# Weight halves written by two DMAs in layer A and in the second block

## The chip, the cores and the metric

The kernel runs on one core of a Trainium2 chip. The metric is the device time of one execution in microseconds (us); of a kernel that was run several times the median counts.

The engines and the letters of the profile: PE is TensorE (matrix products; PEld is its loading of stationary operands), DVE is VectorE, ACT is ScalarE, POOL is GpSimd, SP is SyncE, which here only issues DMAs. A DMA that an engine issues stands in that engine's queue and moves data by itself; SP's DMAs go through queue q1 (hardware_dynamic on the page), GpSimd's through q0 (software_dynamic).

## The reference, cut to what matters

One sequence of S = 512 tokens of width D = 1024, float32 throughout, goes through three blocks:

```
def first_block(x, ...):                       # DEPTH = 2
    for i in range(2):
        mix = dsa_mixer(h, ...) if i == 0 else gla_mixer(h, ...)       # layer A, layer B
        h = layer_norm(DN_ALPHA * h + mix, ...)
        h = layer_norm(DN_ALPHA * h + square(relu(h @ w_up)) @ w_down, ...)   # MLP0, MLP1

def dsa_mixer(x, ...):                         # layer A
    proj = x @ w_in                            # 1024 x 2120: q, k, v, iq, ik, iw
    ... rotate q, k, iq, ik; score = sum_h iw * relu(iq . ik); keep the 128 best keys of each query
    p = softmax(q . k over the kept keys);  o = p @ v
    return o @ w_o                             # 1024 x 1024

def second_block(x, c, ...):
    h = modulate(rms_norm(x), ...)
    proj = h @ w_in                            # 1024 x 2832: q, k, v, mLSTM q and k, v, o, gates
    y_attn = axial attention(q, k, v);  y_mem = bidirectional mLSTM(...)
    x = x + g1 * (concatenate([y_attn, y_mem]) @ w_out)                # 1024 x 1024
    x = x + g2 * ((silu(h @ w_gate) * (h @ w_up)) @ w_down)            # the FFN
    return rms_norm(x)
```

`dsa_mixer`'s two matrices and `second_block`'s `w_in` and `w_out` are the ones that the change touches.

## The kernel before, in words

TensorE's fast path takes a rounded float32 (F32R). To keep float32 precision each operand `x` of a projection is held as two rounded parts, `hi = round(x)` and `lo = x - hi`, and a projection is three products: `hi*hi + hi*lo + lo*hi`. The activations' parts are `xT_hi` and `xT_lo` (line names), the weights' parts `wh` and `wl`.

A weight load takes a tile of 128 partitions x 2048 columns (1 MB; some are smaller) in three steps. SP issues a DMA of the raw float32 weights into a buffer of tag "raw" (name `wr`; L129 in `wcols`, L104 in `wraw`, which `wheads` uses for `w_o` and `w_out`). Then `wsplit` (L107) works in two pieces: ScalarE copies the raw weights to F32R (`wh`, L88), VectorE subtracts (`wl = wr - wh`, L85). The tags raw, wh and wl have two buffers each. As soon as a load's split has read its raw buffer, the next load but one can be fetched into it: raw weights lie ready some time before the split can run, and the split waits for a free pair `wh`, `wl`, that is until PE has made the last product with the pair's load before.

The program runs layer A (`layer_a`, L457), MLP0, layer B (`gla`, `gate_out`), MLP1, the second block (`second`, L1005) and its `ffn`. In layer A the projections are run as steps (`proj_steps`, L146): tokens in 4 tiles of 128, two at a time, and the 1024 rows of the weights in 2 loads of 512 rows; iq's columns first (its first load comes with x through `load_x`), then k with ik and iw (328 columns, "k chunk" below), V (256), Q0 and Q1 (512 each), interleaved with index scores, the selection and attention; at the end `w_o` in 4 loads. The second block does likewise: VM (mLSTM's v), AQ, KV (272 columns), C (four loads of 256 columns, all 1024 rows), OG, then `w_out` in 4 loads.

The order of the instructions on each engine is fixed before the run by a scheduler, from priorities and from when it reckons that operands are there. What stands under `net.urgent()` (loads and splits) gets priority over everything else, in program order among itself. An engine then works its list strictly in order: what stands behind an instruction that waits, waits too. That holds for the DMA issues of SP and of GpSimd as well.

Of the kernel before, what the change touches and what calls it, by code (L numbers as in the profile page):

```python
# [10 lines left out]
F32 = mybir.dt.float32  # L11
F32R = mybir.dt.float32r
I32 = mybir.dt.int32
AF = mybir.ActivationFunctionType
ALU = mybir.AluOpType
# [11 lines left out]
P = 128  # L27
# [10 lines left out]
class Net:  # L38
    def __init__(self, ctx, tc, ins, out):
        self.tc, self.nc, self.ins, self.out = tc, tc.nc, ins, out  # L40
        nc = self.nc
        self.cp = ctx.enter_context(tc.tile_pool(name="cp", bufs=1))
        self.wp = ctx.enter_context(tc.tile_pool(name="wp", bufs=2))
        self.sp = ctx.enter_context(tc.tile_pool(name="sp", bufs=4))
        self.pp = ctx.enter_context(tc.tile_pool(name="pp", bufs=2, space=PSUM))
        self.new_xt()
        self.xh = self.cp.tile([P, KB, S], F32R, name="xT_hi")
        self.xl = self.cp.tile([P, KB, S], F32R, name="xT_lo")
        self.ident = self.cp.tile([P, P], F32, name="ident")
        make_identity(nc, self.ident)  # L50
        self.identr = self.cp.tile([P, P], F32R, name="identr")
        nc.vector.tensor_copy(self.identr, self.ident)
        self.epst = {}
        self.nurgent = 0

    def new_xt(self):
        self.xt = self.cp.tile([P, NT, D], F32, tag="xt", name="x_tok")
# [37 lines left out]
        return self.pp.tile([P, 512], dt, tag=tag, bufs={"a": 3, "t": 2, "s": 2, "o": 1}[tag], name="ps_" + tag)  # L95


    def wraw(self, srcs, kb, n, name="w"):

        with self.urgent():  # L100
            raw = self.wp.tile([P, 2048], F32, tag="raw", name=name + "r")[:, : kb * n]
            rv = raw.rearrange("p (k n) -> p k n", k=kb)
            for psl, ap in srcs:
                self.nc.sync.dma_start(rv[psl], ap)  # L104
        return raw, rv
# [15 lines left out]
    def wcols(self, w, r0, kb, cols):  # L121

        n = sum(m for _, m in cols)
        with self.urgent():
            raw = self.wp.tile([P, 2048], F32, tag="raw", name="wr")[:, : kb * n]
            rv = raw.rearrange("p (k n) -> p k n", k=kb)
            o = 0
            for c0, m in cols:
                self.nc.sync.dma_start(rv[:, :, o : o + m], w[r0 : r0 + kb * P, c0 : c0 + m].rearrange("(k p) n -> p k n", p=P))  # L129
                o += m  # L130
        return self.wsplit(raw, kb, n)

    def wchunk4(self, w, r0, c0):
        return self.wchunk(w, r0, 4, c0, 512)

    def wheads(self, w, r0, c0):

        raw, _ = self.wraw([(slice(64 * b, 64 * b + 64), w[r0 + b * 256 : r0 + b * 256 + 256, c0 : c0 + 512]
                             .rearrange("(r d) n -> d r n", d=64)) for b in range(2)], 4, 512)
        return self.wsplit(raw, 4, 512)  # L140

    def proj_tok(self, *args, **kw):
        for _ in self.proj_steps(*args, **kw):
# [312 lines left out]

def layer_a(net, first):  # L457
    nc, tc, I = net.nc, net.tc, net.ins
    w_in, w_o = I["a_w_in"][0], I["a_w_o"][0]
    xk = net.xk()  # L460
    with tc.tile_pool(name="da", bufs=1) as da:
# [6 lines left out]
        v = da.tile([P, NT, 4, 64], F32, name="v")  # L468
# [175 lines left out]
def mlp(net, i, extra, mod=None):  # L644

    nc, tc, I = net.nc, net.tc, net.ins
    w_up, w_dn = I["mlp_w_up"][i], I["mlp_w_down"][i]
    with tc.tile_pool(name="ml", bufs=1) as mp:
        st = mp.tile([P, NT, 2, 6], F32, name="st")
        hid, rows = [], []  # L650
        NG = 8

        def hidden():
            hid.append([mp.tile([P, 2, S], F32R, tag=x, name=x, bufs=3) for x in ("hh", "hl")])
            return hid[-1]

        def ev_up(j, ps):
            hh, hl = hidden() if j % 2 == 0 else hid[-1]
            r = mp.tile([P, S], F32, tag="eo", name="relu", bufs=2)
            nc.scalar.activation(r, ps, AF.Relu)  # L660
            nc.scalar.activation(r, r, AF.Square)
            net.split(hh[:, j % 2, :], hl[:, j % 2, :], r)

        def up(c):
            e = net.proj_seven(mp, w_up, c * 256, xs, AF.Relu)
            hh, hl = hidden()
            for v, sc in ((e[:, 1], 1.0), (e[:, 2:4], -1.0)):
                nc.scalar.activation(v, v, AF.Relu, scale=sc)
            nc.scalar.activation(e, e, AF.Square)
            v = e.rearrange("p (f t) n -> p f (t n)", f=2)  # L670
            net.split(hh, hl, v)

        def ev_dn(c, n, t, ps):
            sl = slice(n * 512, (n + 1) * 512)
            x = net.xt[:, t, sl]
            if c == 0:
                nc.vector.scalar_tensor_tensor(x, x, ALPHA, ps, op0=ALU.mult, op1=ALU.add)
            else:
                nc.vector.tensor_tensor(x, x, ps, op=ALU.add)
            if c == 2 * NG - 2:  # L680
                net.ln_stats(net.xt[:, t, :], st[:, t], n)
                if n == 1:
                    net.ln_tile(net.xt[:, t, :], st[:, t], t, rows[0][:, 0], rows[0][:, 1], mod is None)
                    if mod is not None:
                        rms_mod(net, mp, t, rows[0][:, 2], rows[0][:, 3], hm=rows[1][:, t], jtag="eo")

        net.proj_pairs([(w_up, 2 * i * P, lambda b, ps, i=i: ev_up(2 * i + b, ps)) for i in range(2)])
        xs = net.x_sums(mp)
        net.proj_feat(w_up, 512, 2, ev_up)
        for g in range(1, NG):  # L690
            if g > 1:
                up(2 * g)
            for n in range(2):
                down_half(net, w_dn, 2 * g - 2, 2 * g, n, hid, ev_dn)
            up(2 * g + 1)
            if g in (1, 3, 5):
                extra[g // 2](mp)
        rows += [mp.tile([P, NT, D], F32, tag=tag, name="rows_" + tag) for tag in ("th", "tl")]
        for n, r in enumerate([I["ln_mlp_g"][i], I["ln_mlp_b"][i]] + [net.mod[m] for m in mod or ()]):
            net.bcast_row(rows[0][:, n], r)  # L700
        down_last(net, mp, w_dn, 2 * NG - 2, hid, ev_dn)
# [3 lines left out]
def layer_b(net):  # L705
# [14 lines left out]
def gla(net, y, ssq):  # L720
# [284 lines left out]
def second(net):  # L1005
# [2 lines left out]
    w_in, w_out = I["w_in_2"][0], I["w_out_2"][0]  # L1008
    H = 4
    xk = net.xk()  # L1010
    with tc.tile_pool(name="sm", bufs=1) as sm:
        qk = sm.tile([P, 8, S], F32, name="mqk")
        v1 = sm.tile([P, NT, H, P + 2], F32, name="mv")
# [6 lines left out]
        with tc.tile_pool(name="sa", bufs=1) as sa:  # L1020
# [3 lines left out]
            v = sa.tile([P, NT, 2, 64], F32, name="av")  # L1024
# [498 lines left out]
```

## Time and profile before

| | us |
|---|---|
| median of 3 runs | 1858.94 (1856.1 to 1861.33) |
| the profiled execution | 1859.66 |
| its span in the profile | 1857.9 |
| PE busy | 1815.5 (98%) |
| DVE busy | 1440.5 (78%) |
| ACT busy | 912.3 (49%) |
| POOL busy | 19.0 (1%) |

The span runs from the first to the last instruction of the execution; 1.8 us of the execution lie around it. Layer A takes the span's first 245 us or so, MLP0 begins at 251, the second block's mixing runs from about 1190 to 1497. In the rows below, an instruction's row gives its start, its duration, engine, line, operation, `output<-inputs`, shape, type, and `xN` where N like ones follow each other directly; `[0.59 <-ACT hst L88]` is idle time ahead of it and what ended that. Windows give the busy time of each engine in a stretch with the number of instructions, then PE's granted clock as a share of full speed, the DMA engines' busy share and GB/s.

### The profile page before, as it was taken

The page shows a single profiled execution, that of the slowest core. Times are in us where ns is not written, and L with a number is a line of the kernel's source. Part 1 is how long each engine was busy: PE and PEld are TensorE (multiplying, and loading weights), DVE is VectorE, ACT ScalarE, POOL GpSimd, SP SyncE. Part 2 cuts the span into 40 slices and gives each one's busy share as a digit, 9 for nine tenths or more (in the row PEclk, how much of TensorE's full clock was granted, in tenths as well). Part 3 has the DMA queues.
Part 4 walks back from the last instruction along what each step waited for, and adds up shares of the span by engine and source line. Part 5 has one row for each costly group of instructions (what it writes and reads, how often), then busy time and mean ns, then how long its engine had stood idle before and what let it go on. Part 6 is the DMA issues. An engine that isn't in the chain of part 4 may idle for free.

```text
span 1857.9 us, 26802 instructions
## 1 busy us (share of the span) xinstructions
PE 1815.5 (98%) x10564; PEld 1532.8 (83%) x10564; DVE 1440.5 (78%) x2467; ACT 912.3 (49%) x1600; POOL 19.0 (1%) x46
## 2 busy tenths in 40 slices
PE   8999999999999999999999999999999899999997
PEld 7865698988888888889888888777566689999996
DVE  5998589878678587468988777877876787788877
ACT  5568644444443544334544444445677445344334
POOL 0010000000000100000000000000000000000000
PEclk9999999999999999999999999999999999999999
DMA  4231244634324222126454323422112122333232
GB/s 143 91 68 52 67 139 158 207 117 148 103 91 134 61 69 69 68 91 188 140 180 140 113 92 111 139 73 81 46 41 69 45 91 68 114 114 114 79 104 91
DMA packets 127161, 190.80 MB, mean 103 GB/s; under 512 B 9279, under 2 KB 77835, under 8 KB 127036
## 3 DMA queue, kind: packets, MB, share of 16 engines
q1 hardware_dynamic: 126996, 189.03, 32.0%
q8 instruction: 83, 1.36, 0.3%
q14 instruction: 42, 0.34, 0.1%
q0 software_dynamic: 32, 0.07, 0.0%
q10 hardware_dynamic: 8, 0.00, 0.0%
HBM read 186.96 MB, written 2.12 MB: 102 GB/s over the span
## 4 chain that ended last, share of the span: by engine, by line
PE 92%; DVE 5%; ACT 2%; issue 0%; DMA 0%; POOL 0%; SPq 0%; DVEq 0%; ACTq 0%; POOLq 0%
PE ps_a L77 51%; PE ps_s L77 15%; PE ps_t L77 11%; PE ps_o L77 7%; PE ps_t L443 1%; PE ps_t L302 1%; PE ps_s L806 1%; PE ps_a L1275 1%; DVE wl L85 1%; PE ps_t L405 1%; PE ps_s L1241 1%; ACT prob L434 0%; PE ps_s L843 0%; PE ps_o L858 0%; ACT wh L88 0%
## 5 line engine op out<-in xcount | busy, mean ns | idle before, releaser
L88 ACT ACTIVATE wh<-wr 128x1024 fp32r<-128x1024 f32 (+2 forms) x284 | 258.6, 958 | 239.3 <-PE ps_t L77 113.3
L85 DVE TENSOR_TENSOR wl<-wr,wh 128x1024 fp32r<-128x1024 f32 (+2 forms) x284 | 304.1, 1104 | 84.6 <-ACT wh L88 55.1
L77 PE MATMUL ps_a<-wh,xT_hi 128*128 128x512 f32 (+3 forms) x536 | 205.3, 387 | 3.6 <-ACT xT_hi L88 2.2
L77 PE MATMUL ps_a<-wh,xT_lo 128*128 128x512 f32 (+3 forms) x536 | 204.3, 385 | 0.6 <-DVE xT_lo L85 0.6
L88 ACT ACTIVATE wsh<-wr 128x1024 fp32r<-128x1024 f32 x94 | 97.5, 1059 | 184.3 <-DVE wr L254 155.5
L77 PE MATMUL ps_a<-xT_hi,wh 128*128 128x256 f32 (+1 forms) x528 | 163.4, 321 | 0.9 <-DVE gtok L1097 0.5
L77 PE MATMUL ps_a<-xT_lo,wh 128*128 128x256 f32 (+1 forms) x528 | 162.7, 319 | 0.0
L77 PE MATMUL ps_a<-xT_hi,wl 128*128 128x256 f32 (+1 forms) x528 | 147.0, 319 | 0.0
L77 PE MATMUL ps_a<-wl,xT_hi 128*128 128x512 f32 (+3 forms) x536 | 143.6, 381 | 0.0
L77 PE MATMUL ps_s<-wh,hh 128*128 128x512 f32 x344 | 136.6, 397 | 0.1
L77 PE MATMUL ps_s<-wh,hl 128*128 128x512 f32 x344 | 136.7, 397 | 0.0
L77 PE MATMUL ps_a<-tl,wsh 128*128 128x256 f32 x528 | 132.1, 283 | 0.0
L77 PE MATMUL ps_a<-th,wsh 128*128 128x256 f32 x528 | 132.1, 282 | 0.0
L77 PEld LDWEIGHTS ps_a<-wh,xT_hi 128*128 128x128 f32 x536 | 101.5, 189 | 25.0 <-issue 4.5
L85 DVE TENSOR_TENSOR wsl<-wr,wsh 128x1024 fp32r<-128x1024 f32 x94 | 113.0, 1221 | 10.7 <-ACT wsh L88 10.7
L77 PEld LDWEIGHTS ps_a<-wh,xT_lo 128*128 128x128 f32 x536 | 101.5, 189 | 19.8 <-DVE xT_lo L85 1.4
L77 PE MATMUL ps_t<-wh,hl 128*128 128x512 f32 x296 | 117.4, 397 | 0.0
L77 PE MATMUL ps_t<-wh,hh 128*128 128x512 f32 x296 | 117.4, 396 | 0.0
L77 PEld LDWEIGHTS ps_a<-wl,xT_hi 128*128 128x128 f32 x536 | 95.6, 188 | 19.3 <-issue 1.6
L77 PEld LDWEIGHTS ps_a<-xT_hi,wh 128*128 128x128 f32 x528 | 100.1, 190 | 9.3 <-issue 0.8
L77 PEld LDWEIGHTS ps_a<-xT_lo,wh 128*128 128x128 f32 x528 | 100.0, 189 | 7.8 <-issue 0.8
L77 PEld LDWEIGHTS ps_a<-tl,wsh 128*128 128x128 f32 x528 | 100.3, 190 | 0.0
(437 smaller groups left out, 4122.3 us busy)
## 6 DMA issues: line engine op xcount, KB each, us to landing
wr<-in_mlp_w_up_dram SPq DMA_DIRECT2D x32, 1024.0 KB
wr<-in_mlp_w_down_dram SPq DMA_DIRECT2D x32, 1024.0 KB
mod_raw<-in_w_ada_dram SPq DMA_DIRECT2D x48, 512.0 KB
wr<-in_b_w_in_dram SPq DMA_DIRECT2D x12, 1024.0 KB
wr<-in_w_gate_dram SPq DMA_DIRECT2D x11, 1024.0 KB
wr<-in_w_up_dram SPq DMA_DIRECT2D x11, 1024.0 KB
wr<-in_w_in_dram SPq DMA_DIRECT2D x10, 1024.0 KB
wr<-in_w_down_dram SPq DMA_DIRECT2D x10, 1024.0 KB
```

What stands on the lines that cost most here:

```text
L77: self.nc.tensor.matmul(ps, lt, rt, start=first, stop=last)
L85: (eng or self.nc.vector).tensor_tensor(out, x, hi.bitcast(F32), op=ALU.subtract)
L88: self.nc.scalar.activation(out, x, AF.Copy)
L302: self.nc.tensor.transpose(ps[:, j * P : (j + 1) * P], src[:, j * P : (j + 1) * P], self.ident)
L405: nc.tensor.transpose(ps[:, j * P : (j + 1) * P], st[:, j0 + j, :], net.identr)
L443: nc.tensor.transpose(pst[:, kb * P : (kb + 1) * P], pr[:, kb * P : (kb + 1) * P], net.ident)
L806: nc.tensor.matmul(ps[:, c * 64 : c * 64 + 64], x[:, c * C : (c + 1) * C], xv[:, c * m : (c + 1) * m, 1, :], start=True, stop=True)
L1241: nc.tensor.matmul(ps, qk[:, 4 + h, a * P : (a + 1) * P], qk[:, h, :], start=True, stop=True)
L1275: nc.tensor.matmul(o, ws[a][:, b * P : (b + 1) * P], v1[:, a, h, 0:129], start=n == 0, stop=n == len(as_) - 1)
```

## The change

`wcols` and `wheads` now hand their sources to a new function `wload`. Where `net.adding` is false it does what was done before. Where it is true, GpSimd issues a DMA that reads the float32 weights from DRAM and writes them as F32R to `wh` (L113); ScalarE writes `-wh` to `wl` in one instruction (L114); GpSimd issues a second DMA that reads the same weights from DRAM again and adds them to `wl` (L116). SP and VectorE have no part. Two of three such loads take their pair from the tags wh and wl; each third takes both from the tag raw, which such loads no longer need for raw weights: three pairs in turn.

```diff
+    def wload(self, srcs, kb, n):
+        v = lambda x: x.rearrange("p (k n) -> p k n", k=kb)
+        with self.urgent():
+            if not self.adding:
+                raw = self.wp.tile([P, 2048], F32, tag="raw", name="wr")[:, : kb * n]
+                for psl, cs, ap in srcs:
+                    self.nc.sync.dma_start(v(raw)[psl, :, cs], ap)
+                return self.wsplit(raw, kb, n)
+
+            self.nadd += 1
+            wh, wl = (self.wp.tile([P, 2048], F32R, tag="raw" if self.nadd % 3 == 0 else x, name=x)[:, : kb * n] for x in ("wh", "wl"))
+            for psl, cs, ap in srcs:
+                self.nc.gpsimd.dma_start(v(wh)[psl, :, cs], ap)
+            self.nc.scalar.activation(wl, wh.bitcast(F32), AF.Copy, scale=-1.0)
+            for psl, cs, ap in srcs:
+                self.nc.gpsimd.dma_start(v(wl)[psl, :, cs], ap, accum_op=ALU.add)
+        return v(wh), v(wl)
...
     def wcols(self, w, r0, kb, cols):
-        with self.urgent():
-            raw = self.wp.tile([P, 2048], F32, tag="raw", name="wr")[:, : kb * n]
...
-                self.nc.sync.dma_start(rv[:, :, o : o + m], w[r0 : r0 + kb * P, c0 : c0 + m].rearrange("(k p) n -> p k n", p=P))
-        return self.wsplit(raw, kb, n)
+            srcs.append((slice(None), slice(o, o + m), w[r0 : r0 + kb * P, c0 : c0 + m].rearrange("(k p) n -> p k n", p=P)))
+        return self.wload(srcs, kb, n)
...
     def wheads(self, w, r0, c0):
-        raw, _ = self.wraw(...)
-        return self.wsplit(raw, 4, 512)
+        return self.wload(...)
...
 def layer_a(net, first):
+    net.adding = True
...
 def mlp(net, i, extra, mod=None):
+    net.adding = False
...
 def second(net):
+    net.adding = True
...
 def ffn(net):
+        net.adding = False
```

`mlp` sets the flag to false ahead of layer B and nothing sets it to true there, so layer B's loads are as before. Changed are 29 loads: 13 of layer A (all but the first of iq) and 16 of the second block. VectorE's list goes from 2421 to 2363 instructions, ScalarE's from 1467 to 1438, SP's from 317 to 278, GpSimd's from 51 to 129; loads with two sources (k, KV, `w_o`, `w_out`) need two DMAs for each half.

The order on SP, from its first DMAs to MLP0's first loads (`wr_243` is iq's second load, `wr_369` and `wr_404` the k chunks; `wr_2901` and `wr_2911` MLP0's first two); before:

```order
L1423 DMA x_tok_67<-in_x_dram 128x512 x6
L129 DMA wr_243<-in_a_w_in_dram 128x4x512
L129 DMA wr_369<-in_a_w_in_dram 128x4x256
L129 DMA wr_369<-in_a_w_in_dram 128x4x72
L309 DMA inv_186<-in_inv_a_dram 128x8
...
L104 DMA wr_2693<-in_a_w_o_dram 64x4x512 x2
L547 DMA x_tok_2233<-in_x_dram 128x1024 x4
L129 DMA wr_2901<-in_mlp_w_up_dram 128x8x256
```

and after (`wr_2868` is MLP0's first load):

```order
L1444 DMA x_tok_67<-in_x_dram 128x512 x6
L326 DMA inv_186<-in_inv_a_dram 128x8
L565 DMA x_tok_2208<-in_x_dram 128x1024 x4
L326 DMA ln_g_2569<-in_ln_mix_g_dram 128x1024
L326 DMA ln_b_2570<-in_ln_mix_b_dram 128x1024
L107 DMA wr_2868<-in_mlp_w_up_dram 128x8x256
```

Layer A's weight loads have left SP's list between x and MLP0. They stand on GpSimd's, here from the program's start to Q1's first load (243/244 is iq's second load, 399/400 the second k chunk in the tag raw, 366/367 the first k chunk, 650/651 and 681/682 V, 864/865 and 895/896 Q0, 1364/1365 Q1); after:

```order
L113 DMA wh_243<-in_a_w_in_dram 128x4x512
L113 DMA wh_399<-in_a_w_in_dram 128x4x256
L113 DMA wh_399<-in_a_w_in_dram 128x4x72
L482 AFFINE_SELECT caus_162<-caus_162 128x128
L116 DMA wl_244<-in_a_w_in_dram 128x4x512
...
L113 DMA wh_650<-in_a_w_in_dram 128x4x256
L116 DMA wl_367<-in_a_w_in_dram 128x4x256
L116 DMA wl_367<-in_a_w_in_dram 128x4x72
...
L113 DMA wh_1364<-in_a_w_in_dram 128x4x512
L116 DMA wl_896<-in_a_w_in_dram 128x4x512
```

Before, GpSimd had of these only the AFFINE_SELECT. Each accumulating DMA stands behind the next load's first DMA.

On PE at the k chunks, before (`wh_372`, `wl_373` are the first k chunk's parts, `wh_407` the second's):

```order
L77 MATMUL ps_a_378<-wl_373,xT_hi_68 128x328 x4
L77 MATMUL ps_a_391<-wh_372,xT_hi_68 128x328
...
L77 MATMUL ps_a_391<-wl_373,xT_hi_68 128x328 x4
L77 MATMUL ps_a_378<-wh_407,xT_hi_68 128x328
```

and after (`wh_366`, `wl_367`; `wh_399`):

```order
L78 MATMUL ps_a_386<-wh_366,xT_lo_69 128x328
L78 MATMUL ps_a_490<-wh_366,xT_hi_68 128x328
L422 MATMUL ps_t_354<-identr_75,hst_349 128x128 x4
L422 MATMUL ps_t_360<-identr_75,hst_349 128x128 x4
...
L78 MATMUL ps_a_490<-wh_366,xT_lo_69 128x328
L78 MATMUL ps_a_373<-wl_367,xT_hi_68 128x328 x4
L78 MATMUL ps_a_386<-wl_367,xT_hi_68 128x328 x4
L78 MATMUL ps_a_373<-wh_399,xT_hi_68 128x328
```

Where 8 products with `wh` preceded the first product with `wl`, there are now 24, for three token tiles (`ps_a_373`, `ps_a_386`, `ps_a_490`), and 8 transposes.

## Rows read from the trace of the kernel before

**Rows 1.** The page's first part: busy time, share and count of each engine.

```profile
PE 1815.5 (98%) x10564; PEld 1532.8 (83%) x10564; DVE 1440.5 (78%) x2467; ACT 912.3 (49%) x1600; POOL 19.0 (1%) x46
```

**Rows 2.** Windows of two parts of layer A and of the second block's mixing.

```profile
16.00:100.00 84.00, 84.00 (x499) 73.00 (x498) 67.12 (x193) 47.90 (x97) 0.00 (x0) 1.00 0.28 82
100.00:190.00 90.00, 83.22 (x423) 54.78 (x423) 78.95 (x297) 73.61 (x213) 6.37 (x16) 1.00 0.24 61
1190.00:1497.00 307.00, 289.56 (x1395) 213.95 (x1394) 235.83 (x499) 181.99 (x395) 2.93 (x14) 0.97 0.19 57
```

**Rows 3.** The chain that ended last, by line: 16 to 100 us, then 1190 to 1495.

```profile
by line: PE ps_a L77 74.7%; PE ps_s L77 11.7%; PE ps_t L405 8.8%; DVE wl L85 2.7%; DVE sc L534 1.1%; PE ps_t L302 0.9%; DVE m L533 0.4%
...
by line: PE ps_a L77 50.9%; PE ps_o L77 6.5%; PE ps_a L1275 6.0%; PE ps_s L1241 3.9%; PE ps_s L77 3.7%; PE ps_t L443 3.6%; DVE wl L85 3.2%; PE ps_t L302 1.9%; PE ps_t L77 1.8%; DVE pt L446 1.7%; PE ps_t L405 1.3%; DVE x_tok L326 1.1%; DVE x
```

**Rows 4.** VectorE's weight splits by line: 16 to 250 us, then 1180 to 1500.

```profile
L85 DVE TENSOR_TENSOR wl<-wr,wh 128x1024 fp32r<-128x1024 f32 (+2 forms) x27 | 28.2, 1084 | 7.1 <-ACT wh L88 6.3 <-PE ps_a L77 0.7
...
L85 DVE TENSOR_TENSOR wl<-wr,wh 128x1024 fp32r<-128x1024 f32 (+1 forms) x34 | 38.0, 1159 | 9.4 <-ACT wh L88 8.5 <-PE ps_a L77 0.8
```

**Rows 5.** A 1 MB weight DMA on SP: its issue, and the window in which its bytes move.

```profile
212.15 0.38 SPq L129 DMA_DIRECT2D wr<-in_mlp_w_up_dram  x1
...
213.00:217.00 4.00, 4.00 (x24) 3.16 (x23) 0.54 (x2) 2.77 (x6) 0.00 (x0) 1.00 0.85 265
```

**Rows 6.** The one DMA that GpSimd issues (KB, us to landing), and its window.

```profile
613.10 1.05 POOL L748 DMA_DIRECT2D wn<-in_b_w_in_dram  x1 [469.86 <-DVE al L759]
...
wn<-in_b_w_in_dram POOLq DMA_DIRECT2D x1, 64.0 KB, 3.8
...
613.00:614.00 1.00, 1.00 (x11) 0.98 (x9) 0.87 (x3) 0.74 (x2) 0.90 (x1) 1.00 0.16 43
```

**Rows 7.** ScalarE's copies of two loads to F32R.

```profile
15.42 2.00 ACT L88 ACTIVATE wh<-wr 128x1024 fp32r<-128x1024 f32 x2
...
28.04 1.39 ACT L88 ACTIVATE wh<-wr 128x656 fp32r<-128x656 f32 x2 [0.59 <-ACT hst L88]
```

**Rows 8.** PE's products around four loads and MLP0's start, in order of time.

```profile
27.55 0.40 PE L77 MATMUL ps_a<-wh,xT_lo 128*128 128x512 f32 x1
...
32.23 0.31 PE L77 MATMUL ps_a<-wh,xT_hi 128*128 128x328 f32 x1
...
33.43 0.76 PE L77 MATMUL ps_a<-wl,xT_hi 128*128 128x328 f32 x4
...
36.08 0.85 PE L405 MATMUL ps_t<-identr,hst 128*128 128x128 f32 x8
...
67.68 0.28 PE L77 MATMUL ps_a<-wh,xT_lo 128*128 128x256 f32 x1
...
80.72 1.10 PE L77 MATMUL ps_a<-wl,xT_hi 128*128 128x512 f32 x4
...
245.41 2.02 PE L77 MATMUL ps_a<-wh,oa 128*128 128x512 f32 x8
...
250.98 0.28 PE L77 MATMUL ps_a<-xT_hi,wh 128*128 128x256 f32 x1
...
1220.62 0.40 PE L77 MATMUL ps_a<-wh,xT_lo 128*128 128x512 f32 x1
...
1230.66 0.39 PE L77 MATMUL ps_a<-wh,xT_hi 128*128 128x512 f32 x1
...
1232.53 1.09 PE L77 MATMUL ps_a<-wl,xT_hi 128*128 128x512 f32 x4
...
1241.40 0.40 PE L77 MATMUL ps_a<-wh,xT_lo 128*128 128x512 f32 x1
...
1252.96 0.66 PE L77 MATMUL ps_a<-wl,xT_hi 128*128 128x272 f32 x4
```

**Rows 9.** VectorE's first weight split of the second block, in a layer norm's run.

```profile
1189.58 2.35 DVE L85 TENSOR_TENSOR wl<-wr,wh 128x1024 fp32r<-128x1024 f32 x2
```

**Rows 10.** VectorE's probabilities of layer A: ns shortest/median/longest, time, shapes.

```profile
L438 DVE TENSOR_SCALAR prob<-prob,rcp x32: 267/414/562, 109.4 to 212.9; 128x128 f32<-128x128 f32 x8, 128x256 f32<-128x256 f32 x8, 128x384 f32<-128x384 f32 x8, 128x512 f32<-128x512 f32 x8
```

More of the change, by code (lines that the diff above doesn't have):

```diff
@@ L54, in __init__ @@
         self.nurgent = 0
+        self.adding, self.nadd = False, 0
     def new_xt(self):
@@ L123, in wcols @@
         n = sum(m for _, m in cols)
-        with self.urgent():
-            raw = self.wp.tile([P, 2048], F32, tag="raw", name="wr")[:, : kb * n]
-            rv = raw.rearrange("p (k n) -> p k n", k=kb)
-            o = 0
-            for c0, m in cols:
-                self.nc.sync.dma_start(rv[:, :, o : o + m], w[r0 : r0 + kb * P, c0 : c0 + m].rearrange("(k p) n -> p k n", p=P))
-                o += m
-        return self.wsplit(raw, kb, n)
+        srcs, o = [], 0
+        for c0, m in cols:
+            srcs.append((slice(None), slice(o, o + m), w[r0 : r0 + kb * P, c0 : c0 + m].rearrange("(k p) n -> p k n", p=P)))
+            o += m
+        return self.wload(srcs, kb, n)
     def wchunk4(self, w, r0, c0):
@@ L136, in wheads @@
     def wheads(self, w, r0, c0):
-        raw, _ = self.wraw([(slice(64 * b, 64 * b + 64), w[r0 + b * 256 : r0 + b * 256 + 256, c0 : c0 + 512]
-                             .rearrange("(r d) n -> d r n", d=64)) for b in range(2)], 4, 512)
-        return self.wsplit(raw, 4, 512)
+        return self.wload([(slice(64 * b, 64 * b + 64), slice(None), w[r0 + b * 256 : r0 + b * 256 + 256, c0 : c0 + 512]
+                            .rearrange("(r d) n -> d r n", d=64)) for b in range(2)], 4, 512)
     def proj_tok(self, *args, **kw):
```

## The prediction, made before the changed kernel ran

> **What bounds the kernel now.** I read the page's busy times first, then windows by stage, then the chain of waits by line inside the two stages that change, then single rows of PE, ScalarE, SP and GpSimd around the loads. The page shows PE busy for 98% of the span [rows 1]: everything rests on whether PE's products get their operands a little later or a little earlier. By stage [rows 2], PE has no gap between 16 and 100 us (84.00 of 84); from 100 to 190 us it stands 6.8 us (90 less 83.22), in the second block's mixing 17.4 (307 less 289.56). VectorE is busy for 78.95 of 90 and 235.83 of 307 there. On the chain [rows 3] VectorE's weight split holds 2.7% of 84 us, 2.3 us, and 3.2% of 305 us, 9.8 us: together 12.1 us in which the end of the stage hung on the work that is now taken from VectorE. The other 93% or more of both chains is mostly PE's own work and stays.
>
> **What is removed.** VectorE loses its split: 28.2 us of layer A's and 38.0 of the second block's [rows 4], less some 3 instructions of MLP0's first loads or of the FFN's that the stretches hold. Most of that lay beside PE's work and is worth nothing. What can come back is bounded above by the 12.1 us of the chain and the splits of three loads that fall into 100 to 190 us, where PE stands and VectorE is nearly full: 6 pieces x 1.08 = 6.5 [rows 4], 18.6 in all. It is bounded below by 2.35 us, the one split that stands in the run of a layer norm, with PE's first products of the second block behind it [rows 9]; the other pieces on the chain may only have been the last of several waits. I take 7.2, halfway between 2.35 and 12.1, since a stage whose VectorE is 77 to 88% busy has another VectorE instruction next in line.
>
> **What is added.** ScalarE does one 128x2048 negation for two 128x1024 copies, both over 2048 columns: 2.0 us [rows 7], no change in its busy time. GpSimd gets 78 DMA issues. The one that it issued before held it for 1.05 us [rows 6], so 82 us spread over 550 us of stages in which it was busy for some 9 [rows 2]: no load on the engine. The bytes double, in stages whose DMA engines are 19 to 28% busy [rows 2]; they have room.
>
> What counts is the length of one load's chain. Before, raw weights lay ready, and when the last product with a pair's old content was through, a copy and a subtraction refilled it piece by piece, 2.2 us to the first piece (1.0 and 1.16) [rows 7, 4]. Now from that moment follow a DMA, its landing, the negation and a second DMA, each after the other. On SP 1 MB takes 4.85 us: issued at 212.15, moving until 217 [rows 5], 4.0 of it at 265 GB/s. GpSimd's issue takes 1.05 where SP's takes 0.38 [rows 5, 6]: 5.5 us. The chain of a 1 MB load is then 5.5 + 2.0 + 5.5 = 13.0 us. For the k chunk (0.67 MB in two DMAs) the half is 0.85 to the first byte + 0.67 + 1.05 for the second issue + 2.55 of bytes = 5.1, the chain 5.1 + 1.4 [rows 7] + 5.1 = 11.6; for KV (0.56 MB, two DMAs) 4.7 + 1.1 (2.0 x 1088/2048) + 4.7 = 10.5.
>
> No accumulating DMA is in the trace. From below I bound it by a plain one; it can't be quicker than that, since it reads the same bytes and the old values too. From above I take four times the time for its bytes. Between them stand 1.5 (three streams in place of two: weights in, old values in, sums out) and 2. For 1 MB this adds 2.0 us at 1.5, 4.0 at 2 and 12.0 at four. I take 1.5.
>
> Where does PE wait for it? Most loads have more than such a chain between a pair's release and its first `lo` product; the third pair sees to that. Four do not, by the new order [rows 8]:
> - k chunk, the first: released at 27.95 (27.55 + 0.40); its first `lo` product comes 24 products of 0.15 (eight from 32.23 to 33.43) and 0.85 of transposes after 32.23, at 36.7. Cover 8.7, chain 11.6: 2.9 late at the plain price, 4.2 at 1.5, 5.4 at 2, 10.5 at four.
> - Q0's second: 67.96 to 80.72, cover 12.8, chain 13.0: 0.2, 2.2, 4.2, 12.2.
> - AQ's second: released at 1221.02; 14 products of 0.234 (eight from 1230.66 to 1232.53) from 1230.66 on give 1233.9, cover 12.9: 0.1, 2.1, 4.1, 12.1.
> - KV's second: 1241.80 to 1252.96, cover 11.2, chain 10.5: 0, 0.4, 1.4, 5.6.
>
> Behind a waiting issue GpSimd's list stands: V's first DMA is ahead of the k chunk's accumulation, Q1's ahead of Q0's, KV's ahead of AQ's. Where such a buffer comes free late, the accumulation is late by the same; behind `w_o`'s accumulation stand Q1's rotations, which GpSimd computes and attention waits for. On ScalarE the negation waits for the landing, and the PSUM evacuations behind it wait too. I put no price of its own on these: they hit the same four waits, and four times the price of bytes covers them.
>
> Two edges. At the start 1.68 MB of layer A's first `hi` halves now run beside x instead of behind it on SP; they take 1.68 / 0.265 = 6.3 us of the engines' time if all of it goes ahead of x. From 0 to 6.3 I take 2.5, as x is issued first and only its tail shares the engines. At MLP0's start both raw buffers were free early and its first weights were issued at 212.15 [rows 5]; now one of `w_o`'s pairs lies in the tag raw until its last `hi` product at 247.4 (245.41 + 2.02) [rows 8]. Then 4.85 for the DMA and some 2 us for the first split pieces make 254.3, against a first product at 250.98: 3.3 late, and from 0, if PE has other work to bring forward, to 5, if the two loads' DMAs share the engines. I take 2.5.
>
> **The sum.** Costs at the plain price: 2.9 + 0.2 + 0.1 + 0 + 2.5 + 2.5 = 8.2. At 1.5: 4.2 + 2.2 + 2.1 + 0.4 + 5.0 = 13.9. At 2: 20.1. At four: 45.4. The profiled execution took 1859.66 us (span 1857.9 and 1.8 around it), 0.7 above the median of the runs, 1858.94. 1859.66 + 13.9 - 7.2 = 1866.4, so **1866**. By itself: the Trainium skill, "DMA: Bandwidth & Descriptors", section "Anatomy of one DMA — SWDGE (gpsimd) path", gives 2.0 us + bytes/436e3 for a DMA of GpSimd's, an estimated 4.4 us for 1 MB and 10.8 for the chain; by it the four waits shrink to about 1, and the sum is an estimated 1858 to 1859. The row with 64 KB landed 3.8 us after its issue [rows 6], above the 2.2 of that formula, so I stay with the rows.
>
> **The rivals.**
> - *VectorE's relief wins (faster).* In the second block the splits on the chain go, and PE's 17.4 us of gaps close by up to 9.8; layer A gives 2.3. If accumulation costs as a plain DMA and the edges cost nothing: 3.2 - 12.1 = -8.9, about 1851; with the 18.6, 1844. For it: the chain names the split itself. Against: PE has no gap from 16 to 100 us, where two of the tight loads lie. It decides for faster from the point where the four waits and the edges together cost less than 12 us, a price of bytes under about 1.3.
> - *Costs and relief cancel.* The price 1.5, relief 9 to 14, edges as taken: 1859.66 + 13.9 - 14 to + 13.9 - 9, 1860 to 1864, within 0.3%.
> - *Accumulation is slow.* At four times the bytes' time: 45.4 - 7.2 = +38.2, 1898. For it: nothing in the trace excludes it, and with a chain of 25 us more loads would be late. Against: only that most covers are long.
> - *VectorE holds GpSimd's issues up.* Each of the 12 issues of the four tight loads would wait for one instruction of VectorE like the scaling of probabilities, 0.41 us [rows 10]: 5 us more, 1871. Against it: the issue at 613.10 took 1.05 us while VectorE was busy for 0.87 of that 1 us [rows 6]. The Trainium skill, "SBUF — State Buffer", section "SBUF: two separate sides", states the rule behind it: GpSimd can't write descriptors while VectorE runs certain copies and scalings from SBUF to SBUF. That one row does not show it, whatever the three instructions were.
> - That layer B doesn't change, other than the words of the change say, is in the order and is no matter of chance.
>
> **How the numbers follow.** 0.3% of 1860, 5.6 us, is about what a measurement of this kernel can tell from no change. The forecast, at a price of 1.5 to 2 and relief of 7: 0.40, of which 0.34 beyond 0.3% (its own range 1862 to 1874). Cancel: 0.14. VectorE's relief wins: 0.28. Slow accumulation: 0.13. Held-up issues: 0.05. Slower is 0.34 + 0.13 + 0.05 = 0.52, the same 0.06 + 0.14 = 0.20, faster 0.28. The range must take in both signs: below to 1848, between the rival's 1851 and 1844; above to 1896, close to the price of four; that leaves out under 1 in 10 on either side.
>
> **What will show it.** An accumulating DMA's time from issue to landing against a plain one of GpSimd's: 5.5 and some 7.5 us by the forecast, equal for the first rival, 17 for the slow one. PE's waits at the k chunk's, Q0's, AQ's and KV's first `lo` products: 4.2, 2.2, 2.1, 0.4 us. PE's gap at MLP0's start. PE busy in the second block's mixing: if its idle time falls from 17.4 to under 10, relief has won. GpSimd's issues: 1.05 us each, longer beside VectorE if the fourth rival holds. The forecast is wrong if the four waits don't appear, or if a load with a long cover is late.

## The result and the profile after

The changed kernel took 1883.2 us (median of 4 runs, 1880.8 to 1884.3), the kernel before 1859.1: a ratio of 1.0133 (1.0118 to 1.0147), 24 us slower. The forecast was 1866 with a range of 1848 to 1896: the side is right and the time lies in the range, but it is 17 us later than forecast and outside the 1862 to 1874 that the likeliest case gave itself. The profiled execution took 1880.8, its span is 1879.0, 21.1 more than before.

First the page's busy times of the changed kernel, which answer to [rows 1]:

```profile
PE 1819.0 (97%) x10564; PEld 1537.9 (82%) x10564; DVE 1384.0 (74%) x2409; ACT 905.4 (48%) x1571; POOL 97.1 (5%) x124
```

PE does the same 10564 products. It is busy 3.5 us longer and idle 17.6 us longer (60.0 for 42.4). VectorE is 56 us lighter, GpSimd 78 us heavier. Windows of the changed kernel, columns as in [rows 2]; the mixing of its second block runs from 1193 to 1518:

```profile
16.00:100.00 84.00, 73.52 (x427) 63.59 (x427) 42.24 (x138) 41.53 (x79) 18.29 (x17) 0.96 0.69 130
100.00:190.00 90.00, 87.42 (x454) 61.81 (x453) 76.64 (x306) 69.77 (x198) 18.49 (x30) 1.00 0.58 101
1193.00:1518.00 325.00, 301.78 (x1452) 225.50 (x1452) 218.22 (x491) 183.53 (x387) 42.01 (x51) 0.97 0.56 110
```

From 16 to 100 us PE had no gap before; now it has 10.5 us of them, and its granted clock falls to 0.96. From 100 to 190 us, where VectorE was nearly full, the gap shrinks from 6.8 to 2.6. In the mixing it grows from 17.4 to 23.2. So both sides of the sum are there: what VectorE's relief gives back after 100 us, and what late weights take elsewhere. The chain of waits of the changed kernel, 1193 to 1518 us, by line, which answers to [rows 3]; VectorE's split is gone from it, and DMAs of both halves and ScalarE's negation (L114) stand there:

```profile
by line: PE ps_a L78 36.2%; issue 8.5%; DMA wh<-in_w_in_dram 8.3%; PE ps_o L78 5.6%; PE ps_a L1295 5.1%; PE ps_t L460 4.2%; PE ps_s L78 4.0%; DMA wh<-in_w_out_dram 3.1%; ACT wl L114 2.8%; DMA wl<-in_w_in_dram 2.7%; PE ps_s L1261 2.2%; PE ps
```

PE's rows at the places of [rows 8], changed kernel (in brackets the idle time ahead and what ended it):

```profile
26.42 1.17 PE L78 MATMUL ps_a<-wl,xT_hi 128*128 128x512 f32 x4 [1.13 <-DMA wl<-in_a_w_in_dram]
...
46.92 2.53 PE L78 MATMUL ps_a<-wl,xT_hi 128*128 128x328 f32 x8 [4.08 <-DMA wl<-in_a_w_in_dram]
...
98.41 1.20 PE L78 MATMUL ps_a<-wl,xT_hi 128*128 128x512 f32 x4 [3.00 <-DMA wl<-in_a_w_in_dram]
...
264.68 0.38 PE L78 MATMUL ps_a<-xT_hi,wh 128*128 128x256 f32 x1 [2.10 <-ACT wh L89]
...
1257.76 2.04 PE L78 MATMUL ps_a<-wl,xT_hi 128*128 128x512 f32 x4 [6.21 <-DMA wl<-in_w_in_dram]
...
1280.52 0.73 PE L78 MATMUL ps_a<-wl,xT_hi 128*128 128x272 f32 x4 [0.23 <-DMA wl<-in_w_in_dram]
```

These are iq's second load, the first k chunk, Q0's second load, MLP0's start, AQ's and KV's second loads. The forecast named all but the first, with 4.2, 2.2, 2.5, 2.1 and 0.4 us. The DMAs, as the changed kernel's page and its answer on DMAs give them (KB each, median us from issue to landing):

```profile
wh<-in_a_w_in_dram POOLq DMA_DIRECT2D x5, 1024.0 KB, 5.7
wl<-in_a_w_in_dram POOLq DMA_DIRECT2D x5, 1024.0 KB, 8.8
...
wh<-in_a_w_in_dram POOLq DMA_DIRECT2D x4, 512.0 KB, 4.4
wl<-in_a_w_in_dram POOLq DMA_DIRECT2D x4, 512.0 KB, 7.5
...
wh<-in_w_in_dram POOLq DMA_DIRECT2D x2, 32.0 KB, 4.5
wl<-in_w_in_dram POOLq DMA_DIRECT2D x2, 32.0 KB, 7.8
```

In these rows an accumulating DMA lands 3.1 to 3.3 us later than a rounding one of the same size, whether it has 32 KB or 1 MB (the small ones follow a larger one directly in the queue). For the ten 1 MB loads of the second block's `w_in` it is 1.9 later, for the rounding ones take longer there:

```profile
wh<-in_w_in_dram POOLq DMA_DIRECT2D x10, 1024.0 KB, 7.0
wl<-in_w_in_dram POOLq DMA_DIRECT2D x10, 1024.0 KB, 8.9
```

e3 below gives the cleaner comparison, the same DMA at the same place without the adding. The forecast had put a price on bytes, +2.0 at 1 MB and little for small ones. GpSimd's issues, first a rounding and then an accumulating one of 1 MB:

```profile
57.63 0.77 POOL L113 DMA_DIRECT2D wh<-in_a_w_in_dram  x1 [13.88 <-PE ps_t L422]
...
63.38 1.29 POOL L116 DMA_DIRECT2D wl<-in_a_w_in_dram  x1 [0.22 <-ACT kst L89]
```

0.77 and 1.29 us where 1.05 was taken for both [rows 6].

### The profile page after: what moved, and what is told of

Same layout as the page of the kernel before. It is cut to its first block, busy times and chain, and to the rows that moved or that the text cites. A ratio compares the mean times of both kernels' runs of the same rounds, so it can differ in the third digit from the quotient of the medians.

```text
span 1879.0 us, 26805 instructions
## 1 busy us (share of the span) xinstructions
PE 1819.0 (97%) x10564; PEld 1537.9 (82%) x10564; DVE 1384.0 (74%) x2409; ACT 905.4 (48%) x1571; POOL 97.1 (5%) x124
## 4 chain that ended last, share of the span: by engine, by line
PE 80%; issue 6%; DMA 5%; DVE 5%; ACT 2%; POOL 1%; SPq 0%; POOLq 0%; ACTq 0%; DVEq 0%
PE ps_a L78 44%; PE ps_s L78 13%; PE ps_t L78 10%; PE ps_o L78 6%; PE ps_t L460 2%; DMA wh<-in_w_in_dram 1%; PE ps_s L825 1%; PE ps_t L319 1%; DVE wl L86 1%; DMA wl<-in_a_w_in_dram 1%; PE ps_a L1295 1%; ACT wl L114 1%; DMA mod_raw<-in_w_ada_dram 1%; DMA wh<-in_a_w_o_dram 1%; DMA wh<-in_w_out_dram 1%
## 5 line engine op out<-in xcount | busy, mean ns | idle before, releaser
L89 ACT ACTIVATE wh<-wr 128x1024 fp32r<-128x1024 f32 (+1 forms) x226 | 205.0, 954 | 215.2 <-PE ps_t L78 114.3
L86 DVE TENSOR_TENSOR wl<-wr,wh 128x1024 fp32r<-128x1024 f32 (+1 forms) x226 | 241.5, 1099 | 72.0 <-ACT wh L89 43.6
L89 ACT ACTIVATE wsh<-wr 128x1024 fp32r<-128x1024 f32 x94 | 97.5, 1059 | 184.2 <-DVE wr L271 155.4
L78 PE MATMUL ps_a<-wl,xT_hi 128*128 128x512 f32 (+3 forms) x536 | 149.5, 392 | 14.6 <-DMA wl<-in_a_w_in_dram 8.2
```

The lines of the kernel that those rows point to most:

```text
L78: self.nc.tensor.matmul(ps, lt, rt, start=first, stop=last)
L86: (eng or self.nc.vector).tensor_tensor(out, x, hi.bitcast(F32), op=ALU.subtract)
L89: self.nc.scalar.activation(out, x, AF.Copy)
```

## The experiments

The theory after the result: (a) relieving VectorE is worth far more than the 7 us taken, (b) the chain of a load (DMA, negation, accumulating DMA) costs far more than the 14 us taken, above all by the adding. Rivals: the cost comes from GpSimd's queue and the doubled traffic whatever the second DMA does; relief is worth nothing; the order on the engines did it. Ratios are to the kernel before, run on the same chip.

| kernel | us | ratio (95% interval) |
|---|---|---|
| changed | 1883.2 | 1.0133 (1.0118 to 1.0147) |
| e3 second DMA plain | 1863.1 | 1.0020 (1.0010 to 1.0031) |
| e4 no lo split on VectorE, nothing in its place | 1840.0 | 0.9900 (0.9885 to 0.9915) |
| e1 layer A alone | 1876.8 | 1.0097 (1.0078 to 1.0116) |
| e2 second block alone | 1874.9 | 1.0092 (1.0077 to 1.0107) |
| e8 the same, pairs as in the changed kernel | 1871.0 | 1.0057 (1.0037 to 1.0077) |
| e6 third pair shifted by one load | 1883.7 | 1.0129 (1.0112 to 1.0146) |
| e9 first three loads as before | 1878.2 | 1.0111 (1.0094 to 1.0128) |
| e5 only loads with long cover | 1846.4 | 0.9932 (0.9915 to 0.9948) |
| e10 the same, second DMA plain | 1842.3 | 0.9912 (0.9898 to 0.9927) |
| e7 lo split on GpSimd | 1887.9 | 1.0154 (1.0139 to 1.0169) |

**e3, the adding alone.**

```diff
-                self.nc.gpsimd.dma_start(v(wl)[psl, :, cs], ap, accum_op=ALU.add)
+                self.nc.gpsimd.dma_start(v(wl)[psl, :, cs], ap)
```

> The changed kernel with the second DMA of each load writing instead of adding (the lo parts are then the rounded weights; same order on every engine). In the changed kernel's trace an accumulating DMA of 1 MB landed 8.8 us after its issue, a rounding one 5.7. Theory: the waits shorten by some 3 us each, at iq 1.1, k 3.1, Q0 3.0, AQ 3.1, together 10, and what the clock gives back: 1868 to 1873. Rival (what is late is the issue: GpSimd's list and ScalarE's negation, not the adding): within 3 us of 1883.

Measured: 1863.1, 20 us less. The adding (its landing and GpSimd's longer issue together) is the larger part of the loss over the kernel before, and of more weight than the waits that I had counted (10). Between the two profiles the difference is 16.7 us (1879.0 less 1862.3): 10.7 are idle time of PE, about what was counted, and 6.0 are busy time (1819.0 less 1813.0) for the same products, at a mean granted clock of 0.993 for 0.989. Its DMA rows show the price taken away, at `w_in` of the second block too:

```profile
wl<-in_w_in_dram POOLq DMA_DIRECT2D x10, 1024.0 KB, 5.7
...
wl<-in_a_w_in_dram POOLq DMA_DIRECT2D x5, 1024.0 KB, 5.7
...
wl<-in_a_w_in_dram POOLq DMA_DIRECT2D x4, 512.0 KB, 4.5
```

PE's waits at the k chunk and AQ shrink from 4.08 and 6.21 to 2.01 and 3.23, Q0's is gone:

```profile
45.03 1.96 PE L78 MATMUL ps_a<-wl,xT_hi 128*128 128x328 f32 x8 [2.01 <-DMA wl<-in_a_w_in_dram]
...
1243.96 2.04 PE L78 MATMUL ps_a<-wl,xT_hi 128*128 128x512 f32 x4 [3.23 <-DMA wl<-in_w_in_dram]
```

The order is the same on PE, VectorE, ScalarE and GpSimd, so the order did not make these 20 us.

**e4, the relief alone.** In the kernel before, `wsplit` for the same 29 loads:

```diff
+            if self.nolo:
...
+                    self.hi(wh[:, sl], raw[:, sl])
+                wh = wh.rearrange("p (k n) -> p k n", k=kb)
+                return wh, wh
```

> The kernel before, with VectorE's splits of the same 29 loads left out and nothing put in their place (the products with the lo part read the hi part). Theory: relief of VectorE is worth what the stretch from 115 to 227 us of the changed kernel gave back, 7 us, and some more in the second block: 1847 to 1852. Rival (relief is worth nothing; the changed kernel's PE only caught up on idle time that it had anyway): 1857 to 1860.

Measured: 1840.0, 19.6 us faster. Relief was expected at 7 to 12; it is worth a little more than the prediction's upper bound, 18.6. Of the 17.9 us between the profiles (1857.9 less 1840.0), 12.4 are idle time of PE and 5.5 busy time. Windows of this kernel, its mixing from 1187 to 1479:

```profile
100.00:190.00 90.00, 89.08 (x465) 59.85 (x465) 71.02 (x282) 79.58 (x229) 6.56 (x16) 1.00 0.24 62
1187.00:1479.00 292.00, 283.13 (x1383) 211.34 (x1382) 204.21 (x465) 183.69 (x395) 3.95 (x14) 0.98 0.19 60
```

PE's gaps fall from 6.8 to 0.9 and from 17.4 to 8.9. With e3 this gives the ledger in medians: relief -19.6, two plain DMAs in the load's chain +23 (1863.1 less 1840.0), the adding +20, in all +24. The first two terms are not pure: e4 also takes the subtraction out of each load's chain, and the scheduler gave PE another order than in either of the two kernels. The +23 holds, not taken apart, the longer chain, GpSimd's queue, the doubled traffic, the third pair and the new order; so the rival of the queue and the traffic stays open for its part of that.

**e5 and e10, the price where cover is long.** Only Q1, `w_o`, C, OG and `w_out` are changed, and the third pair is given so that it is free when the next raw weights come:

```diff
+LATE = (*range(8, 14), *range(20, 30))
-            if not self.adding:
+            self.nadd += self.adding
+            if not (self.adding and self.nadd in LATE):
...
-            wh, wl = (... tag="raw" if self.nadd % 3 == 0 else x ...)
+            wh, wl = (... tag="raw" if self.nadd in (9, 11, 20, 24, 27) else x ...)
```

> The change only for loads that have long cover: layer A's Q1 and w_o (6 loads) and the second block's C, OG and w_out (10); the other 13 as before, and the tag raw taken only where it is free early again (no load at the end of layer A or of the mixing). Theory: no wait for a second DMA is left at iq, k, Q0, AQ and KV, nor at MLP0's start, and most of VectorE's relief stays (layer A 5 of 7, second block 9 of 12): 1844 to 1851. Rival (the chain of two DMAs is late at these loads too, or the relief hangs on the loads left out): 1857 or more.

Measured: 1846.4, faster than both kernels, by 12 us (0.7%) than the one before. One wait of PE for a second DMA is left, in its list of waits:

```profile
PE ps_a L80 <- DMA wl<-in_a_w_in_dram: 1.9, 1, 1.9
```

e10 is this kernel with e3's edit:

> The kernel in which only the loads with long cover are changed, with the second DMA writing instead of adding (the lo parts are then the rounded weights; the same order on every engine). In the changed kernel this took 20 us away. Theory (the 3 us that adding costs decide only where a load is tight): within 4 us of the kernel with adding, 1842 to 1847. Rival (adding costs wherever it is done, by the DMA engines' time or GpSimd's longer issue): 1840 or less.

Measured: 1842.3, 4 us less, at the lower edge of what was expected; the intervals of the two ratios overlap. Against the 20 of the changed kernel the adding is cheap here. In the profiles 3.1 of the 3.4 us between the two arise from 98 to 117 us, where e5's one wait stands: Q1's first product comes at 98.2 and 98.1, MLP0's at 247.9 and 244.8, the FFN's at 1482.9 and 1479.4. The other loads with adding cost next to nothing. The price decides where a load is tight.

**e9 and e6, does a wait that is taken away stay away?** In e9 the first three loads (iq's second, both k chunks) are as before:

```diff
-            if not self.adding:
+            self.nadd += self.adding
+            if not self.adding or self.nadd <= 3:
```

> The changed kernel with layer A's first three changed loads (iq's second, k's two) as before. Theory: by k's end the changed kernel was 12.7 us late, 5 by x and iq's second load at the start and 7.7 at k (wait and lower clock); without these three loads this is gone, and Q0's wait of 3 stays: 1869 to 1873. Rival (a wait taken away comes back at the next load, as when the pair was moved by one load, or PE's gaps from 100 to 190 us swallow the gain): 1877 or more.

Measured: 1878.2 (1873.0 to 1880.6), by the median the rival; the rows are of the run at 1873.0. Start and k are nearly as before (k's second chunk is through at 51.1 us, before 50.0), but V's first load, which did not wait in the changed kernel, does now, in this kernel's rows:

```profile
58.78 0.74 PE L78 MATMUL ps_a<-wl,xT_hi 128*128 128x256 f32 x4 [1.81 <-DMA wl<-in_a_w_in_dram]
```

e6 begins the count at 1, so that k's first chunk has the early pair:

```diff
-        self.adding, self.nadd = False, 0
+        self.adding, self.nadd = False, 1
```

> The changed kernel with its count of loads begun at 1: the pair of the tag raw goes to the loads one earlier (k's first chunk and not its second, w_o's third load but one and not the last but one). Theory: a wait hangs on which load gets the pair that is free early; k's first chunk no longer waits (5.0 us), MLP0's raw buffers come free earlier (2.6), AQ's second load waits as before: 1873 to 1877. Rival (any load so early in layer A waits, the wait only moves to the next load): within 3 us of 1883.

Measured: 1883.7, no change, again the rival. The k chunk that waits is now the second, and MLP0's late start is gone but stands at the FFN, whose raw buffers the last `w_out` load now holds:

```profile
49.12 0.84 PE L78 MATMUL ps_a<-wl,xT_hi 128*128 128x328 f32 x4 [3.17 <-DMA wl<-in_a_w_in_dram]
...
1521.76 0.58 PE L78 MATMUL ps_a<-xT_hi,wh 128*128 128x256 f32 x1 [3.76 <-ACT wh L89]
```

**e1, e2 and e8, the two parts.** One line left out each: `net.adding = True` in `second` (e1) or in `layer_a` (e2).

> The change in layer A alone; the second block loads as before. Theory (the long chain of a load, at the few places where a load is tight, costs the time): in the changed kernel's profile layer A's end came 11.5 us later than before, MLP0's start 1.6 more, and 2.9 more fell to layer B under a lower clock: 1872 to 1875 against 1859. Rival (the loss is the second block's, and layer A's delay would be caught up later): 1859 to 1864.

> The change in the second block alone; layer A as before. Theory: the second block's mixing added 5 us in the changed kernel, 1864, with the wait for AQ's second lo part (6.2 us there) in the profile. Rival: the two parts hang together (the third pair, the order): more than 1870, or no later than before, under 1861.

Measured: 1876.8, above the 1872 to 1875 expected, and 1874.9, more than the 1864 expected. Together, +17 and +15 are more than the whole's 24, which for e2 was the rival (the parts hang together). In e2 VM's second load has no third pair, and PE waits for it and for a late layer norm from the first products on:

```profile
1208.07 0.76 PE L78 MATMUL ps_a<-wl,xT_hi 128*128 128x512 f32 x1 [3.46 <-DMA wl<-in_w_in_dram]
```

e8 is e2 with the count begun at 13, so that the pairs fall as in the changed kernel:

> The second block alone again, with the count begun so that its second load (VM's) gets the pair of the tag raw, as in the changed kernel; in the run before it was AQ's first. Theory (the sum of the two parts, 17 + 15, was more than the 24 of the whole because another load got the pair that is free early; PE stood 13.8 us between 1185 and 1250 there, 5.1 in the changed kernel): 1863 to 1868. Rival (the second block alone is dearer for another reason, such as the raw loads on SP): 1873 to 1877.

Measured: 1871.0, between theory and rival; that wait of 3.46 is gone. By the medians the pairs explain some of the surplus (17 + 13 against 24). Most of the rest is no matter of the parts. From the second block on, e8 has the changed kernel's order on PE, VectorE, ScalarE and GpSimd, yet its profiled run took 8.9 us longer from C to the FFN, 6.0 of them busy time at a lower granted clock (first line e8, second the changed kernel):

```profile
1276.48:1508.23 231.75, 219.66 (x1026) 159.32 (x1026) 156.78 (x340) 143.79 (x305) 24.78 (x34) 0.96 0.50 100
```

```profile
1295.05:1517.93 222.88, 213.69 (x1027) 153.38 (x1026) 156.69 (x340) 143.95 (x305) 24.77 (x34) 0.99 0.52 104
```

Of e8's five runs three took 1871.0 to 1871.5 at a mean clock of 0.989 to 0.991, two 1863.7 and 1865.3 at 0.995 and 0.994; with those two the parts would add up to the whole. Likewise e1, in the same order as the changed kernel up to the second block, reached MLP0 at 267.6 us in its profile, the changed kernel at 264.7. Why the clock fell in one execution and not in the other stays open.

**e7, relief without a second DMA.** GpSimd does the subtraction in place of VectorE:

```diff
-                self.split(wh[:, sl], wl[:, sl], raw[:, sl])
+                self.hi(wh[:, sl], raw[:, sl])
+                self.lo(wl[:, sl], raw[:, sl], wh[:, sl], self.nc.gpsimd if self.pool_lo else None)
```

> The kernel before with the subtractions of the same 29 loads done by GpSimd instead of VectorE (raw by SP's DMA and hi by ScalarE as before). VectorE's relief without any second DMA. By the 1.29 us of GpSimd's 128x512 products a piece of 1024 columns takes some 2.5 us where VectorE's took 1.16. Theory: relief of 20 less one to two us at each of the four or five tight loads: 1842 to 1850. Rival (GpSimd and VectorE hold each other up, or the longer pieces put the tight loads late by much more): 1856 or more.

Measured: 1887.9, the rival and a clear miss. GpSimd's pieces of 1024 columns took 2.47 us on the mean, as expected. What was not: VectorE's score sums, 462 to 746 ns before (first row, kernel before; shortest, median, longest), take up to 2639 ns in e7 (second row):

```profile
L525 DVE SCALAR_TENSOR_TENSOR sc<-rl,iws,sc x21: 462/618/746, 54.6 to 80.8; 128x384 f32<-128x384 f32 x7, 128x512 f32<-128x512 f32 x7, 128x256 f32<-128x256 f32 x7
```

```profile
L528 DVE SCALAR_TENSOR_TENSOR sc<-rl,iws,sc x21: 460/619/2639, 60.2 to 91.0; 128x384 f32<-128x384 f32 x7, 128x512 f32<-128x512 f32 x7, 128x256 f32<-128x256 f32 x7
```

The median stays, single ones are held. Two of the 21 are longer than before, and they are the only two that run beside GpSimd's pieces (GpSimd's row, then VectorE's, e7):

```profile
74.81 8.00 POOL L86 TENSOR_TENSOR wl<-wr,wh 128x1024 fp32r<-128x1024 f32 x3 [16.81 <-ACT wh L89]
...
75.13 2.64 DVE L528 SCALAR_TENSOR_TENSOR sc<-rl,iws,sc 128x512 f32<-128x512 f32 x1
...
78.16 2.43 DVE L528 SCALAR_TENSOR_TENSOR sc<-rl,iws,sc 128x512 f32<-128x512 f32 x1
```

The Trainium skill, "SBUF — State Buffer", section "SBUF: two separate sides", says that VectorE, where it has two inputs in SBUF, and GpSimd, where it reads SBUF, take an SBUF port pair by an exclusive lock and that the later one is blocked for the other's whole instruction; a longest time that grows by 1.9 us, beside pieces of 2.47, agrees. How much of e7's 48 us over e4 is this and how much the longer pieces was not taken apart.

## Why the prediction was right or wrong, step by step

**The side and the bound: right, the nearness of the number luck.** PE waits for weights; that it would be slower, and at which loads, came out. But the relief was taken 12 us too small and the costs 29 us too small; that the time still lies in the range is because the two errors have opposite signs.

**The relief: mis-sized, the step "I take 7.2, halfway between 2.35 and 12.1".** It is 19.6 (e4). The reason given, that VectorE would have another instruction next in line, did not hold where PE stood: its gaps from 100 to 190 us fell from 6.8 to 0.9. The bound above, the chain's share plus the three loads' splits at 100 to 190 us, was the better reading.

**The costs: mis-sized, 13.9 for what e4 and the result put at 43.** Where they fall is seen from the start of the first product with a load's `wh`, us, in four profiles (after and e3 have the same order):

| first product of | before | after | e3 | e4 | after less e4 |
|---|---|---|---|---|---|
| k | 32.2 | 38.3 | 38.5 | 33.5 | 4.8 |
| V | 49.9 | 62.5 | 59.8 | 51.3 | 11.2 |
| Q0 | 71.6 | 85.4 | 82.5 | 72.7 | 12.7 |
| Q1 | 97.5 | 115.3 | 109.5 | 98.6 | 16.7 |
| MLP0 | 251.0 | 264.7 | 257.6 | 243.9 | 20.8 |
| VM | 1192.8 | 1213.9 | 1201.5 | 1187.6 | 26.3 |
| AQ | 1225.1 | 1242.5 | 1231.7 | 1217.8 | 24.7 |
| KV | 1249.0 | 1275.6 | 1260.5 | 1241.7 | 33.9 |
| C | 1266.3 | 1295.4 | 1277.5 | 1256.3 | 39.1 |
| FFN | 1496.6 | 1517.9 | 1500.9 | 1478.6 | 39.3 |

The last column's steps against the forecast's terms: start 4.8 for 2.5, k 6.4 for 4.2, Q0 4.0 for 2.2, from Q1 to MLP0 4.1 for 2.5, AQ 9.2 for 2.1, KV 5.2 for 0.4. Not forecast: V 1.5, and 5.5 between MLP0 and VM (1.6 of them in layer B, at the end of this document). Between VM and AQ 1.6 come back. After C nothing is lost: there covers are long.

These steps are not waits alone. Windows from the first product of k to that of V, AQ to KV and KV to C, changed kernel and then e4:

```profile
38.29:62.54 24.25, 20.17 (x124) 19.40 (x125) 4.92 (x24) 9.15 (x19) 4.80 (x5) 0.86 0.54 94
1242.52:1275.60 33.08, 26.87 (x114) 21.34 (x112) 8.80 (x21) 10.12 (x15) 8.14 (x10) 0.85 0.61 112
1275.60:1295.42 19.82, 17.04 (x122) 16.02 (x121) 13.50 (x54) 11.01 (x30) 4.78 (x5) 0.91 0.87 141
```

```profile
33.45:51.25 17.80, 17.71 (x125) 16.93 (x124) 6.30 (x29) 9.93 (x23) 0.00 (x0) 1.00 0.18 46
1217.82:1241.65 23.83, 23.83 (x113) 19.34 (x112) 10.29 (x27) 9.83 (x17) 0.00 (x0) 1.00 0.33 91
1241.65:1256.30 14.65, 14.65 (x121) 14.32 (x120) 10.66 (x43) 11.57 (x30) 0.00 (x0) 1.00 0.25 75
```

At k PE's idle time grows by 4.0 us, as forecast, and its busy time by 2.5: the same products at a mean granted clock of 0.86, between the levels of 1.2 and 2.4 GHz, instead of 1.00. At AQ 6.2 are the wait and 3.0 the clock. At KV the wait for its second load is 0.23, where 0.4 was forecast: 2.4 are the clock, and the idle time of 2.8 is in the main another wait, in PE's list of waits:

```profile
PE ps_t L422 <- DVE qst L1101: 2.2, 1, 2.2
```

In all, of the 39.0 us between the two profiles (1879.0 less 1840.0), 30.0 are idle time of PE (60.0 for 30.0) and 9.0 busy time (1819.0 for 1810.0). The forecast had no term for the clock.

- *The price of the adding* was taken in proportion to bytes, 1.5. Against e3's plain DMA at the same place it is 3.0 to 3.4 us for the loads of `w_in` from 32 KB to 1 MB and for `w_out`'s 1 MB, so nearly fixed, but 1.7 and 0.9 for the 512 KB halves of `w_o` and `w_out`; e3 takes 20 us away.
- *"They have room"*, the DMA engines: their busy share from 16 to 100 us went from 0.28 to 0.69, and a rounding DMA of 1 MB took 7.0 us in the second block where layer A's took 5.7 and the forecast had 5.5. What this costs is part of the +23 above.
- *The chain of AQ's second load* was put at 13.0 + 2.0. In the changed kernel it is 18.5 from GpSimd's issue at 1239.26 to PE's product at 1257.76. GpSimd's rows:

```profile
1239.26 0.77 POOL L113 DMA_DIRECT2D wh<-in_w_in_dram  x1 [3.38 <-PE ps_a L78]
1242.06 1.49 POOL L113 DMA_DIRECT2D wh<-in_w_in_dram  x2 [2.03 <-PE ps_a L78]
1248.86 3.98 POOL L116 DMA_DIRECT2D wl<-in_w_in_dram  x3 [5.30 <-ACT wl L114]
```

  and ScalarE's, where the negation begins as AQ's `hi` has landed:

```profile
1246.64 2.92 ACT L114 ACTIVATE wl<-wh 128x2048 fp32r<-128x2048 f32 x2 [3.31 <-DMA wh<-in_w_in_dram]
```

  The `hi` half took 7.4 us and not 5.5, with KV's two `hi` DMAs issued behind it at 1242.06; then 2.2 to the accumulating issue at 1248.86, and 8.9 to PE. The cover was 12.3 (to 1251.55, where PE stopped), near the 12.9 of the forecast; the chain was what was mis-sized.
- *"I put no price of its own on these"*, the queues behind a waiting instruction: this was the step that missed VM's start. ScalarE waits 8.07 us for a `hi` half to land, negates, and only then loads its table for the layer norm's root (1.28 us) and computes the root (L337), for which VectorE waits 3.01 us and PE, in the end, 2.60. In the kernel before that table load stood at 1174.18, ahead of the root's operand, and held up nothing. ScalarE's rows, then VectorE's and PE's, changed kernel:

```profile
1198.42 1.92 ACT L114 ACTIVATE wl<-wh 128x2048 fp32r<-128x2048 f32 x1 [8.07 <-DMA wh<-in_w_in_dram]
1200.35 1.28 ACT L337 ACT_TABLE_LOAD   x1
1201.64 0.30 ACT L337 ACTIVATE sd<-mv,c 128x1 f32<-128x1 f32 x1
...
1201.97 0.16 DVE L339 RECIPROCAL rs<-sd 128x1 f32<-128x1 f32 x1 [3.01 <-ACT sd L337]
...
1208.54 0.66 PE L319 MATMUL ps_t<-ident,rows_tl 128*128 128x128 f32 x4 [2.60 <-DVE rows_tl L1000]
```

- *Each tight load by itself against the times of before*: e6 and e9 show that a saved wait is not simply saved. A wait that goes brings PE to the next load earlier, and that load's chain isn't done either.
- *The edges*: x beside the first `hi` halves cost 4.8 for 2.5; the wait for MLP0's raw buffers 2.10 for 2.5. (The 1.68 MB of the first are 1.72 in the unit of the rate beside it; only a bound rested on that.) e6 moved the second one to the FFN.

**The rivals.** Relief (a gain of up to 18.6) and slow accumulation (45 at four times) both came true in size, against each other. The mechanism of the second did not: an accumulating DMA of 1 MB landed after 8.8 us, near the forecast's 7.5 and far from the 17 of that rival. The plain price would not have won: e3 is at 1.0020, not at 1851. That VectorE holds GpSimd's issues up did not show in layer A: the 11 accumulating issues of `w_in` took 1285 to 1834 ns with a median of 1294. In the second block its 14 took 1272 to 2226 with a median of 1421; what lengthened some of them was not looked into. The estimate of 10.8 us for the chain, by the Trainium skill's formula in "DMA: Bandwidth & Descriptors", section "Anatomy of one DMA — SWDGE (gpsimd) path", was further off than the rows: a rounding DMA of 1 MB took 5.7 us, not 4.4.

## What to carry to other kernels

Before work is moved from a busy engine to a chain of DMAs, write down for each place how long the chain is from the buffer's release, and use it only where the cover is longer; e5 did that and was faster where the whole change was slower. For what relief is worth, the chain's share together with the work that is taken out of the stretch where PE stood (18.6) came close here, 19.6; the halfway value did not. A wait can cost more than its own length: against e4 the changed kernel paid 30.0 us in PE's idle time and 9.0 in its busy time. An instruction that waits for a DMA holds up all that stands behind it on its engine: look at what that is before it is costed at nothing.

## What the runs showed of the hardware that was not expected

An accumulating DMA of GpSimd's landed 3.0 to 3.4 us later than a plain one at the same place (e3), from 32 KB to 1 MB; for 512 KB halves of `w_o` and `w_out` it was 1.7 and 0.9. It held GpSimd for 1.29 us instead of 0.77 at 1 MB.

PE's granted clock falls in stretches that the change does not touch. Layer B, the same 62 products, in the kernel before and then in the changed one:

```profile
629.00:645.00 16.00, 16.00 (x62) 11.13 (x61) 6.07 (x14) 13.30 (x14) 0.97 (x1) 1.00 0.20 66
```

```profile
642.00:661.00 19.00, 19.00 (x62) 12.93 (x61) 9.13 (x22) 14.33 (x16) 1.30 (x1) 0.82 0.18 56
```

PE is busy throughout in both and takes 3 us longer at a mean of 0.82, between its levels of 1.2 and 2.4 GHz. In e3 and e4 the same products took 17.6 and 17.5 us. Ahead of it PE had worked without gaps worth naming in both kernels; why the clock fell in one of them stays open.
